# GpSimd joins the engines that keep the program's order in the attention loop of a transformer block

## The chip, the cores and the metric

The kernel runs on one core of one Trainium2 chip. The metric is the device time of one launch in microseconds (us); it is taken three times and the median counts. A core has five engines that run at the same time, each with an instruction queue of its own that it works through from front to back: TensorE (PE: matmuls and transposes, with PEld for its weight loads), VectorE (DVE), ScalarE (ACT), GpSimd (POOL) and SyncE (SP, which here only issues DMAs). Where one instruction needs another engine's result, it waits at the head of its queue for a semaphore, and all that stands behind it in that queue waits too.

## The reference

One transformer block on 1024 tokens of width 1024 in float32: a gated linear recurrence and a differential attention side by side, a projection of both, and an expert-choice mixture of experts. The part that this document is about is the attention and the projection behind it:

```python
def block(args):
    qi, start = args
    qpos = start + jnp.arange(Q_BLOCK, dtype=jnp.int32)
    bias = bias_table[t5_buckets(kpos[None, :] - qpos[:, None])].astype(jnp.float32)
    bias = bias.transpose(2, 0, 1)
    s = jnp.einsum('bqhjd,bkhjd->bhjqk', qi, k).astype(jnp.float32) + bias[None, :, None]
    p = jax.nn.softmax(s, axis=-1)
    w = (p[:, :, 0] - lam * p[:, :, 1]).astype(v.dtype)
    return jnp.einsum('bhqk,bkhd->bqhd', w, v)
...
o = rms_norm(o, g_o) * (1.0 - lam_init)
...
mix = jnp.dot(jnp.concatenate([y_lru, y_att], axis=-1), w_out[l])
x = x + gate1 * mix
```

There are 4 heads and 8 blocks of 128 queries for each, and two score matrices (j = 0, 1) for each block.

## The kernel before, in words

The program comes in stages: modulation and the first norm, input projections with the recurrence, the attention, the output projection with the second norm and the router's logits, the search for the experts' tokens, and the experts themselves. Float32 products are made of parts: an operand is split into a high part (ScalarE copies it) and a low part (the rest, by a subtraction), and TensorE multiplies the parts.

The attention loop (line 907 on) has NG + 2 = 34 iterations g. Its body is a software pipeline over 32 units (a unit is one head and one block of queries). In iteration g:

- TensorE transposes the weights of unit g-2 into two PSUM banks (`w_tr`, tile pw, line 814), multiplies the weights of unit g-3 with v (`pv_mm`, tile pv), and makes the scores of unit g+1 in two halves (`sc_mm`, tile sc), in the order pw, sc half 0, pv, sc half 1.
- VectorE adds the bias and finds the extremum of unit g's two halves (`sc_max`, line 768), and between them brings the two probability matrices of unit g-1 together (`comb0` line 798, `comb1` line 803, `comb2` line 807).
- ScalarE empties the two pw banks into tile wt (`w_evac`), and takes the two exponentials of unit g (`sc_exp`). `comb0` of a unit needs its second exponential, and the next transposes need the pw banks empty.

Every four units a tile of outputs is complete. `o_evac` (g = 6, 10, ...) has ScalarE copy it to tile o and GpSimd square it (osq, line 837). Two iterations later (g = 8, 12, ...) `o_rstd` has VectorE sum the squares (hov, line 845) and begin an inverse square root (hoy, lines 852 and 853), and GpSimd finish it with three Newton steps of four small instructions (hot and hoy, lines 855 to 858) and scale o with the result (line 861). At g = 10, 14, ... `o_out` transposes o on TensorE (tile po).

Into the same loop the preparation of the output projection is laid, one block k of 128 rows of w_out at g = 4, 8, 12, 16, 24, 26, 28 and 30 (`load_wo`): a DMA on SP's queue brings the block into a tile wo of a ring of five buffers, GpSimd multiplies it by the gate in four pieces (line 886), ScalarE copies the product to its high part (who, wx0o or wos, through `act`, line 90), and GpSimd subtracts that to get the low part (wlo, wx1o or wos, line 890). For the first tokens the projection starts in iteration 33, after the last scores.

What order an engine's instructions take is decided when the program is built. By default a scheduler goes by its own estimates of time and puts on each engine what it thinks is ready first. Within `tc.manual_schedule(engines=...)` the engines that are named take the order in which the Python code issues their instructions; here these are PE, DVE and ACT for the attention loop. GpSimd's and SP's instructions of the loop are placed by the scheduler.

Of the kernel before, what the change touches and what calls it, by code (L numbers as in the profile page):

```python
# [82 lines left out]
def tile_block(ctx: ExitStack, tc, x, cols, w_mod, b_mod, w_in, wa, wx, lam_qk, relT, w_out, g2, w_router,  # L83
# [639 lines left out]
    def prep_begin(h):  # L723
        sets = {}

        def load(tg, kind, parts):
            t_ = sets[tg] = qk_tile(f"{tg}{h}", F32R) if h else qk0[f"{tg}0"]
            for j in range(2):
                for a in range(2):
                    SY.dma_start(out=t_[j].bitcast(F32)[64 * a:64 * a + 64, :], in_=qkd[kind, h][parts[a], 64 * j:64 * j + 64, :])  # L730

        def bias():
            bt = sets["b"] = ap.tile([P, 1920], F32, name=f"bias{h}", tag="bias", bufs=1) if h % 2 else \
                qk_one("c", f"bias{h}", F32, [P, 1920]) if h else qk0["bias0"]
            src = bvd[h, 0:1920]
            SY.dma_start(out=bt, in_=bass.AP(tensor=src.tensor, offset=src.offset, ap=[[1, P], [1, 1920]]))

        qs, kh, kl = ("qs", 0, (0, 1)), ("kh", 1, (0, 0)), ("kl", 1, (1, 1))
        if h:
            for q in (qs, kh, kl):  # L740
                load(*q)
            bias()
        else:
            load(*kh)
            load(*kl)
            load(*qs)
            bias()
        prs[h] = (sets["b"], [sets[tg] for tg in ("qs", "kh", "kl")])
# [4 lines left out]
    def sc_mm(g, j):  # L753
        h, qt = divmod(g, NT)
        qs, kh, kl = (t_[j] for t_ in prs[h][1])
        sc_ = psa.tile([P, S], F32, tag="sc", bufs=2, name=f"sc{g}_{j}") if g > 1 else \
            psb.tile([P, S], F32, tag="pg", bufs=2, name=f"sc{g}_{j}")
        for i, kk in enumerate((kh, kl)):
            for n in range(2):
                mm(sc_[:, n * 512:(n + 1) * 512], qs[:, qt * P:(qt + 1) * P], kk[:, n * 512:(n + 1) * 512], i == 0, i == 1)  # L760
        scp[g, j] = sc_

    def sc_max(g, j):
        h, qt = divmod(g, NT)
        p_ = ap.tile([P, S], F32, tag="p", bufs=NPB, name=f"p{g}_{j}") if g > 1 else \
            raw_tile(f"p1_{j}", [P, S]) if g else p0[j]
        b0 = (NT - 1 - qt) * P
        V.tensor_tensor_reduce(out=p_, in0=scp[g, j], in1=prs[h][0][:, b0:b0 + S], op0=ALU.add, op1=ALU.min, scale=1.0,  # L768
                               scalar=3.0e38, accum_out=st_(g)[:, j:j + 1])
        pt_[g, j] = p_  # L770

    def sc_exp(g, j):
        h, qt = divmod(g, NT)
        act(pt_[g, j], pt_[g, j], AF.Exp, scale=-1.0, bias=st_(g)[:, j:j + 1], accum_out=s_sum[:, h, qt, j:j + 1])
# [21 lines left out]
    def comb0(g):  # L796
        h, qt = divmod(g, NT)
        V.reciprocal(out=st_(g)[:, 2:3], in_=s_sum[:, h, qt, 1:2])

    def comb1(g):  # L800
        h, qt = divmod(g, NT)
        r1 = st_(g)[:, 2:3]
        V.tensor_scalar(out=r1, in0=r1, scalar1=nlam, scalar2=s_sum[:, h, qt, 0:1], op0=ALU.mult, op1=ALU.mult)

    def comb2(g):
        r1 = st_(g)[:, 2:3]
        V.scalar_tensor_tensor(out=pt_[g, 0], in0=pt_[g, 1], scalar=r1, in1=pt_[g, 0], op0=ALU.mult, op1=ALU.add)

    def w_tr(g):
        for kq in range(2):  # L810
            pw = psa.tile([P, 512], F32, tag="pw", bufs=2, name=f"pw{g}_{kq}")
            for b in range(4):
                kt = kq * 4 + b
                T.transpose(pw[:, b * P:(b + 1) * P], pt_[g, 0][:, kt * P:(kt + 1) * P], ident)  # L814
            pvs[g, kq] = pw

    def w_evac(g):
        wts[g] = ap.tile([P, KT, P], F32, tag="wt", bufs=3, name=f"wt{g}")
        for kq in range(2):
            act(wts[g][:, kq * 4:kq * 4 + 4, :], pvs[g, kq].rearrange("p (b q) -> p b q", b=4))  # L820

    def pv_mm(g):
        n, i = divmod(g, 4)
        if i == 0:
            pvs["pv", n] = psa.tile([P, 4, P], F32, tag="pv", bufs=1, name=f"pv{n}")
        for kt in range(KT):
            mm(pvs["pv", n][:, i, :], wts[g][:, kt, :], vt[g // NT][:, kt, :], kt == 0, kt == KT - 1)
# [12 lines left out]
    def o_rstd(n):  # L840
        h, f = divmod(n, 2)
        o, sq = ots[n]
        v, t_, y = (xt_[f"ho{c}"] if n == 7 else ap.tile([P, 4], F32, tag=f"ho{c}", bufs=2, name=f"ho{c}{n}") for c in "vty")
        s0 = s_sum[:, h, f * 4:f * 4 + 4, 0]
        V.tensor_reduce(out=v, in_=sq, op=ALU.add, axis=AX.X)
        V.scalar_tensor_tensor(out=t_, in0=s0, scalar=EPS, in1=s0, op0=ALU.mult, op1=ALU.mult)
        V.scalar_tensor_tensor(out=v, in0=v, scalar=1.0 / P, in1=t_, op0=ALU.mult, op1=ALU.add)
        if h == NH - 1:
            act(y, v, AF.Sqrt)
            V.reciprocal(out=y, in_=y)  # L850
        else:
            V.tensor_scalar(out=y.bitcast(I32), in0=v.bitcast(I32), scalar1=1, scalar2=None, op0=ALU.logical_shift_right)
            V.tensor_scalar(out=y.bitcast(I32), in0=y.bitcast(I32), scalar1=-1, scalar2=0x5F3759DF, op0=ALU.mult, op1=ALU.add)
            for _ in range(3):
                G_.tensor_tensor(out=t_, in0=y, in1=y, op=ALU.mult)
                G_.tensor_tensor(out=t_, in0=t_, in1=v, op=ALU.mult)
                G_.tensor_scalar(out=t_, in0=t_, scalar1=-0.5, scalar2=1.5, op0=ALU.mult, op1=ALU.add)
                G_.tensor_tensor(out=y, in0=y, in1=t_, op=ALU.mult)
        for i in (slice(0, 4),) if h == NH - 1 else (slice(0, 2), slice(2, 4)):
            yb = y[:, i].unsqueeze(2).to_broadcast([P, i.stop - i.start, P])  # L860
            (V if h == NH - 1 else G_).tensor_tensor(out=o[:, i], in0=o[:, i], in1=yb, op=ALU.mult)
# [30 lines left out]
    def mix_mm(pm_, ns, k, yh, yl):  # L892
        mm(pm_, yh, woh[k][:, ns], k == 0, False)
        mm(pm_, yh, wol[k][:, ns], False, False)
        return mm(pm_, yl, woh[k][:, ns], False, k == KT - 1)
# [8 lines left out]
    gate1 = ap.tile([P, 1024], F32, name="gate1")  # L904
    src = modd[0][:, 0:1024]
    SY.dma_start(out=gate1, in_=bass.AP(tensor=src.tensor, offset=src.offset, ap=[[0, P], [1, 1024]]))
    with tc.manual_schedule(engines={mybir.EngineType.PE, mybir.EngineType.DVE, mybir.EngineType.Activation}):
        for g in range(NG + 2):
            hn, u = divmod(g, 8)
            if u == 0 and hn + 1 < NH:  # L910
                prep_begin(hn + 1)
            if g >= 2:
                w_tr(g - 2)
                w_evac(g - 2)
            if 1 < g < NG:
                sc_max(g, 0)
            if 1 <= g <= NG:
                comb0(g - 1)
            n, st = divmod(g - 8, 4)
            if st == 0 and 0 <= n < 6:  # L920
                o_rstd(n)
            if g < NG:
                if g > 1:
                    sc_exp(g, 0)
                if 0 < g < NG - 1:
                    sc_mm(g + 1, 0)
                if g > 1:
                    sc_max(g, 1)
            if 1 <= g <= NG:
                comb1(g - 1)  # L930
            if 1 < g < NG:
                sc_exp(g, 1)
            if 1 <= g <= NG:
                comb2(g - 1)
            if 3 <= g <= NG:
                pv_mm(g - 3)
            if g == NG:
                pv_mm(NG - 2)
            if 0 < g < NG - 1:
                sc_mm(g + 1, 1)  # L940
            if g in (4, 8, 12, 16, 24, 26, 28, 30):
                load_wo({4: 0, 8: 1, 12: 2, 16: 3, 24: 4, 26: 5, 28: 6, 30: 7}[g])
            n, st = divmod(g - 6, 4)
            if st == 0 and 0 <= n < 7:
                o_evac(n)
            n, st = divmod(g - 10, 4)
            if st == 0 and 0 <= n < 6:
                o_out(n)
            if g == NG + 1:
                o_rstd(6)  # L950
                mix0 = psa.tile([P, 1024], F32, tag="sc", bufs=2, name="mix0")
                for n in range(2):
                    ns = slice(n * 512, (n + 1) * 512)
                    for k in range(NCT):
                        mix_mm(mix0[:, ns], ns, k, y0[:, 0, k, :], y0[:, 1, k, :])
                o_out(6)
                pv_mm(NG - 1)
# [506 lines left out]
```

## Time and profile before

| | |
|---|---|
| median of 3 runs | 1181.63 us (1180.05 to 1181.79) |
| the profiled execution's own time | 1183.49 us |
| its span, first to last instruction | 1181.8 us |
| busy: PE, DVE, ACT, POOL | 1116.1, 955.8, 791.3, 481.7 us |
| attention loop in this span | about 315 to 475 us |
| experts in this span | from about 602 us on |

The span is what the profile shows; the time of the same execution is 1.7 us longer. A row of the timeline gives the start, the duration of a run of equal instructions, engine, line, operation, out<-in with the sizes, how many, and, in brackets, how long the engine had stood idle before and what ended that. Buffer numbers are left out of names there.

### The profile page before, as it was taken

The page shows a single profiled execution, that of the slowest core. Times are in us where ns is not written, and L with a number is a line of the kernel's source. Part 1 is how long each engine was busy: PE and PEld are TensorE (multiplying, and loading weights), DVE is VectorE, ACT ScalarE, POOL GpSimd, SP SyncE. Part 2 cuts the span into 40 slices and gives each one's busy share as a digit, 9 for nine tenths or more (in the row PEclk, how much of TensorE's full clock was granted, in tenths as well). Part 3 has the DMA queues.
Part 4 walks back from the last instruction along what each step waited for, and adds up shares of the span by engine and source line. Part 5 has one row for each costly group of instructions (what it writes and reads, how often), then busy time and mean ns, then how long its engine had stood idle before and what let it go on. Part 6 is the DMA issues. An engine that isn't in the chain of part 4 may idle for free.

```text
span 1181.8 us, 17872 instructions
## 1 busy us (share of the span) xinstructions
PE 1116.1 (94%) x6320; PEld 937.7 (79%) x6320; DVE 955.8 (81%) x1242; ACT 791.3 (67%) x1046; POOL 481.7 (41%) x540
## 2 busy tenths in 40 slices
PE   6999899999979999999569999999999999999996
PEld 4698898798869899777447888888888888888885
DVE  6897657875569896543679999999999999999995
ACT  7548282295467787543328887878888787888784
POOL 4693132133086646344534324444323444332400
PEclk9999999999999999999769999999999999999999
DMA  9765625704781505425799999999999999999911
GB/s 334 228 198 177 220 84 170 242 18 112 193 242 45 150 19 180 162 107 211 266 342 330 363 386 380 390 391 402 378 394 393 369 392 410 394 394 386 393 37 18
DMA packets 146994, 304.34 MB, mean 258 GB/s; under 512 B 16973, under 2 KB 43725, under 8 KB 146901
## 3 DMA queue, kind: packets, MB, share of 16 engines
q1 hardware_dynamic: 135008, 279.99, 65.7%
q0 software_dynamic: 5488, 19.45, 6.4%
q10 hardware_dynamic: 6408, 3.77, 1.1%
q8 instruction: 50, 0.82, 0.3%
q14 instruction: 40, 0.32, 0.1%
HBM read 277.95 MB, written 25.21 MB: 257 GB/s over the span
## 4 chain that ended last, share of the span: by engine, by line
PE 75%; DVE 7%; issue 5%; POOL 5%; DMA 5%; ACT 2%; SPq 1%; POOLq 0%; ACTq 0%; DVEq 0%
PE ab L93 28%; PE y L93 13%; PE mix L93 7%; PE pjz L93 4%; PE pjk L93 3%; PE sc L93 3%; PE pjv L93 3%; PE pv L93 3%; PE pw L814 2%; DMA wr<-in_w_mod_dram 2%; POOL wo L886 2%; PE pg L93 1%; DVE macc L623 1%; DMA wo<-in_w_out_dram 1%; PE pf L1348 1%
## 5 line engine op out<-in xcount | busy, mean ns | idle before, releaser
L1248 POOL TENSOR_SCALAR oh<-iot,slot 128x128 bf16<-128x128 bf16 x120 | 146.4, 1234 | 252.5 <-PE pf L1348 252.4
L93 PE MATMUL ab<-wh,xeh 128*128 128x512 f32 x512 | 202.2, 395 | 0.2 <-ACT xeh L90 0.2
L93 PE MATMUL ab<-wh,xel 128*128 128x512 f32 x512 | 199.7, 390 | 0.0
L93 PE MATMUL ab<-wl,xeh 128*128 128x512 f32 x512 | 157.7, 389 | 0.0
L93 PEld LDWEIGHTS ab<-wl,xeh 128*128 128x128 f32 x512 | 96.1, 188 | 20.4
L93 PEld LDWEIGHTS ab<-wh,xel 128*128 128x128 f32 x512 | 96.2, 188 | 19.5 <-DVE xel L1261 0.5
L93 PEld LDWEIGHTS ab<-wh,xeh 128*128 128x128 f32 x512 | 96.1, 188 | 19.5 <-ACT xeh L90 0.5
L141 DVE TENSOR_TENSOR wl<-w_0r,wh 128x1024 fp32r<-128x1024 f32 x79 | 96.8, 1226 | 10.2 <-ACT wh L90 0.4
L90 ACT ACTIVATE wh<-w_0r 128x1024 fp32r<-128x1024 f32 x81 | 86.1, 1062 | 24.8 <-PE ab L93 14.9
L141 DVE TENSOR_TENSOR wl<-w_3r,wh 128x1024 fp32r<-128x1024 f32 x79 | 96.7, 1225 | 6.2
L90 ACT ACTIVATE wh<-w_1r 128x1024 fp32r<-128x1024 f32 x79 | 83.5, 1058 | 23.7 <-PE ab L93 18.9
L90 ACT ACTIVATE wh<-w_3r 128x1024 fp32r<-128x1024 f32 x79 | 83.9, 1062 | 22.0 <-PE ab L93 17.4
L141 DVE TENSOR_TENSOR wl<-w_2r,wh 128x1024 fp32r<-128x1024 f32 x80 | 96.4, 1221 | 2.6 <-ACT wh L90 1.4
L90 ACT ACTIVATE wh<-w_2r 128x1024 fp32r<-128x1024 f32 x80 | 84.7, 1060 | 19.1 <-PE ab L93 18.7
L141 DVE TENSOR_TENSOR wl<-w_1r,wh 128x1024 fp32r<-128x1024 f32 x78 | 92.7, 1220 | 3.9 <-ACT wh L90 2.1
L768 DVE CUSTOM_DVE_ANT_0 p<-sc,bias 128x1024 f32<-128x1024 f32 x64 | 77.7, 1216 | 10.0 <-PE sc L93 9.9
L93 PE MATMUL y<-wh,htl 128*128 128x512 f32 x256 | 82.9, 395 | 0.0
L93 PE MATMUL y<-wh,hth 128*128 128x512 f32 x256 | 80.9, 396 | 0.0
L93 PE MATMUL y<-wl,hth 128*128 128x512 f32 x256 | 79.6, 391 | 0.0
L90 ACT ACTIVATE p<-p,stat 128x1024 f32<-128x1024 f32 x60 | 68.5, 1151 | 9.1 <-DVE stat L768 9.1
L93 PEld LDWEIGHTS pv<-v,wt 128*128 128x128 f32 x512 | 61.7, 192 | 2.5
L93 PE MATMUL pv<-v,wt 128*128 128x128 f32 x512 | 62.1, 275 | 0.0
(459 smaller groups left out, 2862.5 us busy)
## 6 DMA issues: line engine op xcount, KB each, us to landing
w_0r<-in_w_dram SPq DMA_DIRECT2D x81, 512.0 KB, 8.8
w_1r<-in_w_dram SPq DMA_DIRECT2D x79, 512.0 KB, 8.3
w_2r<-in_w_dram SPq DMA_DIRECT2D x78, 512.0 KB, 8.8
w_3r<-in_w_dram SPq DMA_DIRECT2D x77, 512.0 KB, 8.9
wr<-in_w_mod_dram SPq DMA_DIRECT2D x32, 512.0 KB, 4.9
wi<-in_w_in_dram SPq DMA_DIRECT2D x18, 512.0 KB, 4.4
w_5r<-in_w_dram SPq DMA_DIRECT2D x17, 512.0 KB, 8.0
wm<-in_w_mod_dram SPq DMA_DIRECT2D x32, 256.0 KB, 4.8
```

The lines of the kernel that those rows point to most:

```text
L90: return A.activation(out=out, in_=in_, func=func, **kw)
L93: return T.matmul(out, lhsT=lhsT, rhs=rhs, start=start, stop=stop)
L141: return (eng or V).tensor_tensor(out=lo, in0=src, in1=hi.bitcast(F32), op=ALU.subtract)
L623: V.scalar_tensor_tensor(out=macc[i], in0=w, scalar=sc[:, k:k + 1], in1=macc[i], op0=ALU.mult, op1=ALU.add)
L768: V.tensor_tensor_reduce(out=p_, in0=scp[g, j], in1=prs[h][0][:, b0:b0 + S], op0=ALU.add, op1=ALU.min, scale=1.0, scalar=3.0e38, accum_out ...
L814: T.transpose(pw[:, b * P:(b + 1) * P], pt_[g, 0][:, kt * P:(kt + 1) * P], ident)
L886: G_.tensor_tensor(out=r[:, qs], in0=r[:, qs], in1=gate1[:, qs], op=ALU.mult)
L1248: G_.tensor_scalar(out=oh[:, t, :], in0=iot, scalar1=slot[:, e, t:t + 1], scalar2=None, op0=ALU.is_equal)
L1348: T.transpose(pt[:, b * P:(b + 1) * P], sa[:, b * P:(b + 1) * P], ident)
```

## The change

GpSimd is added to the engines that keep the program's own order in the attention loop; nothing else is changed.

```diff
-    with tc.manual_schedule(engines={mybir.EngineType.PE, mybir.EngineType.DVE, mybir.EngineType.Activation}):
+    with tc.manual_schedule(engines={mybir.EngineType.PE, mybir.EngineType.DVE, mybir.EngineType.Activation, mybir.EngineType.Pool}):
         for g in range(NG + 2):
```

The orders of PE, DVE, ACT and SP are the same in both programs; GpSimd's differs in the attention loop alone. The first place is GpSimd's queue around its first work in the loop: the products with the gate (line 886) for blocks k = 0 to 5 (tiles wo0 to wo5), the low part of block 0 (wlo0), and the first squares (osq0); - is before, + is the change.

```order
 L886 TENSOR_TENSOR wo0_3164<-wo0_3164,gate1_3014 128x256 x4
-L886 TENSOR_TENSOR wo1_3385<-wo1_3385,gate1_3014 128x256 x2
 L890 TENSOR_TENSOR wlo0_3167<-wo0_3164,who0_3166 128x256 x4
-L886 TENSOR_TENSOR wo1_3385<-wo1_3385,gate1_3014 128x256 x2
-L886 TENSOR_TENSOR wo2_3593<-wo2_3593,gate1_3014 128x256 x4
-L886 TENSOR_TENSOR wo3_3820<-wo3_3820,gate1_3014 128x256 x4
-L886 TENSOR_TENSOR wo4_4222<-wo4_4222,gate1_3014 128x256 x4
-L886 TENSOR_TENSOR wo5_4315<-wo5_4315,gate1_3014 128x256 x4
 L837 TENSOR_TENSOR osq0_3258<-o0_3257 128x256 x2
 L855 TENSOR_TENSOR hot0_3340<-hoy0_3341 128x4
```

The products of blocks 1 to 5, twenty instructions, leave their place ahead of the first squares.

The second place is the same queue at g = 12, where the inverse square root of output tile 1 ends (line 858, then the scaling of o1) and block 2 is prepared.

```order
 L858 TENSOR_TENSOR hoy1_3549<-hoy1_3549,hot1_3548 128x4
 L861 TENSOR_TENSOR o1_3478<-o1_3478,hoy1_3549 128x256 x2
+L886 TENSOR_TENSOR wo2_3593<-wo2_3593,gate1_3014 128x256 x4
 L890 TENSOR_TENSOR wlo2_3596<-wo2_3593,who2_3595 128x256 x4
-L886 TENSOR_TENSOR wo7_4536<-wo7_4536,gate1_3014 128x256 x4
 L837 TENSOR_TENSOR osq2_3687<-o2_3686 128x256 x2
```

The product of block 2 now stands behind the Newton steps and the scaling of the same iteration, and that of block 7, which stood ahead of the squares of tile 2, is gone from here. At g = 8, 16, 24 and 28 it is alike with blocks 1, 3, 4 and 6; the products of 5 and 7 stand behind the low parts of 4 and 6.

The third place is ScalarE's queue at g = 12 and 13, the same in both programs: who2 reads the product of block 2.

```order
L90 ACTIVATE p12_0_3544,s_sum_2734<-p12_0_3544,stat_2998 128x1024
L90 ACTIVATE p12_1_3575,s_sum_2734<-p12_1_3575,stat_2998 128x1024
L90 ACTIVATE who2_3595<-wo2_3593 128x1024
L90 ACTIVATE wt11_3616<-pw11_0_3606 128x512
L90 ACTIVATE wt11_3616<-pw11_1_3611 128x512
L90 ACTIVATE p13_0_3619,s_sum_2734<-p13_0_3619,stat_2998 128x1024
L90 ACTIVATE p13_1_3628,s_sum_2734<-p13_1_3628,stat_2998 128x1024
```

Nothing moved here: behind who2 stand the emptying of the next pw banks and the exponentials of unit 13.

## Rows read from the trace of the kernel before

**Rows 1.** The page, part 4: the chain that ended last, shares by line.
```profile
PE ab L93 28%; PE y L93 13%; PE mix L93 7%; PE pjz L93 4%; PE pjk L93 3%; PE sc L93 3%; PE pjv L93 3%; PE pv L93 3%; PE pw L814 2%; DMA wr<-in_w_mod_dram 2%; POOL wo L886 2%; PE pg L93 1%; DVE macc L623 1%; DMA wo<-in_w_out_dram 1%; PE pf L1348 1%
```
**Rows 2.** Windows, undisturbed attention; stretch, its length, busy us by engine, clock, DMA.
```profile
400.00:420.00 20.00, 20.00 (x146) 18.38 (x145) 18.52 (x38) 15.97 (x30) 6.17 (x17) 1.00 0.09 28
```
**Rows 3.** Timeline, PE and ACT, g = 3 to 6: who0's wait.
```profile
329.84 1.06 ACT L90 ACTIVATE who<-wo 128x1024 fp32r<-128x1024 f32 x1 [1.80 <-POOL wo L886]
330.40 1.95 PE L93 MATMUL pv<-v,wt 128*128 128x128 f32 x16
...
334.16 0.16 DVE L798 RECIPROCAL stat<-s_sum 128x1 f32<-128x1 f32 x1 [1.43 <-ACT p L90]
...
334.92 1.95 PE L93 MATMUL pv<-v,wt 128*128 128x128 f32 x16
```
**Rows 4.** Timeline around g = 8: POOL, DVE, PE.
```profile
339.36 9.95 POOL L886 TENSOR_TENSOR wo<-wo,gate 128x256 f32<-128x256 f32 x13
...
344.17 1.95 PE L93 MATMUL pv<-v,wt 128*128 128x128 f32 x16
...
350.48 0.69 DVE L845 TENSOR_REDUCE hov<-osq 128x4 f32<-128x512 f32 x1 [7.40 <-POOL osq L837]
...
353.03 1.22 PE L93 MATMUL sc<-kh,qs 128*128 128x512 f32 x2 [6.91 <-DVE stat L768]
...
357.73 1.95 PE L93 MATMUL pv<-v,wt 128*128 128x128 f32 x16
```
**Rows 5.** Timeline around g = 16: DVE and PE.
```profile
389.65 0.69 DVE L845 TENSOR_REDUCE hov<-osq 128x4 f32<-128x512 f32 x1 [1.44 <-POOL osq L837]
...
390.19 1.95 PE L93 MATMUL pv<-v,wt 128*128 128x128 f32 x16
...
395.88 1.95 PE L93 MATMUL pv<-v,wt 128*128 128x128 f32 x16
```
**Rows 6.** Timeline, POOL, DVE and ACT in g = 11 to 13.
```profile
366.12 3.81 POOL L886 TENSOR_TENSOR wo<-wo,gate 128x256 f32<-128x256 f32 x4
...
370.78 0.17 DVE L853 TENSOR_SCALAR hoy<-hoy 128x4 int32<-128x4 int32 x1
...
373.77 1.05 ACT L90 ACTIVATE who<-wo 128x1024 fp32r<-128x1024 f32 x1
...
375.05 1.09 ACT L90 ACTIVATE wt<-pw 128x512 f32<-128x512 f32 x2 [0.23 <-PE pw L814]
...
375.40 1.19 POOL L861 TENSOR_TENSOR o<-o,hoy 128x256 f32<-128x256 f32 x2
```
**Rows 7.** Timeline, ACT, DVE and PE in g = 13 to 15.
```profile
377.15 1.14 ACT L90 ACTIVATE p<-p,stat 128x1024 f32<-128x1024 f32 x1
...
378.74 0.15 DVE L798 RECIPROCAL stat<-s_sum 128x1 f32<-128x1 f32 x1
378.93 1.04 PE L814 MATMUL pw<-ident,p 128*128 128x128 f32 x8
379.13 1.23 DVE L768 CUSTOM_DVE_ANT_0 p<-sc,bias 128x1024 f32<-128x1024 f32 x1 [0.25 <-PE sc L93]
...
380.28 0.27 DVE L803 TENSOR_SCALAR stat<-stat,misc,s_sum 128x1 f32<-128x1 f32 x1
...
380.59 1.29 DVE L807 SCALAR_TENSOR_TENSOR p<-p,stat,p 128x1024 f32<-128x1024 f32 x1
...
382.45 0.70 PE L93 MATMUL sc<-kh,qs 128*128 128x512 f32 x2
...
383.89 1.04 PE L814 MATMUL pw<-ident,p 128*128 128x128 f32 x8
```
**Rows 8.** Windows around gaps of PE; columns as in rows 2, PE busy third, clock after POOL.
```profile
36.40:39.20 2.80, 0.15 (x2) 0.08 (x1) 2.63 (x2) 0.38 (x1) 1.86 (x1) 1.00 1.15 343
39.60:42.90 3.30, 3.30 (x15) 2.07 (x15) 2.26 (x7) 2.48 (x2) 0.22 (x1) 0.50 1.00 324
...
350.20:357.00 6.80, 3.97 (x13) 3.38 (x14) 6.38 (x15) 2.94 (x5) 4.34 (x15) 0.50 0.62 184
...
390.00:394.00 4.00, 3.54 (x24) 2.81 (x23) 3.86 (x10) 3.00 (x6) 2.41 (x7) 1.00 1.04 245
```

## The prediction

> **What bounds the kernel now.** I read the page's chain first, then the attention by windows, then its timeline engine by engine. The chain is TensorE nearly all the way, but one entry of it is GpSimd's: the products with the gate, 2% of the span, with a load of w_out (1%) beside them [rows 1]. That is where the change acts. In an undisturbed part of the loop TensorE is busy for all 20.00 us of 20, VectorE for 18.52, ScalarE for 15.97 and GpSimd for 6.17 [rows 2]: TensorE is the bound, one unit takes 334.92 - 330.40 = 4.52 us from pv to pv [rows 3], and every gap that opens on TensorE here is lost for good, since the experts behind it are a chain of matmuls as well [rows 1].
>
> There are two such gaps now. At g = 8 GpSimd is in a run of gate products (13 of them from 339.36 on, 9.95 us), the first squares stand behind them, VectorE waits 7.40 us for these, and TensorE stands still for 6.91 us [rows 4]. From pv to pv that iteration takes 357.73 - 344.17 = 13.56 us. At g = 16 VectorE waits 1.44 us for squares behind the product of block 7, and the step is 395.88 - 390.19 = 5.69 us [rows 5].
>
> **What the change removes.** In the new order the first squares stand behind block 0 alone, and no squares of tiles 0 to 3 stand behind products of later blocks. Both waits go. Worth: 13.56 - 4.52 = 9.04 us and 5.69 - 4.52 = 1.17 us, together **10.2 us**. It is the same number of instructions on GpSimd; none is added, and no DMA moves, since SP's order is the same. The loads of blocks 6 and 7 wait on SP's queue for the low parts of blocks 1 and 2, which are a few us later relative to their units; behind them stand the keys of head 3, needed only at g = 23, and nothing else before the loop's end, so I cost that at nothing. If that cover were gone, a late key tile would stop the scores once, for a time like its own delay.
>
> **What it adds.** The scheduler had made the products long before ScalarE needs them. In the program's order the product of a block stands behind the Newton steps and the scaling of the same iteration, and these start only when VectorE has done its part (hoy). ScalarE's order is unchanged, so its copy who now reaches the head of its queue before the product exists, and behind it stand the emptying of the pw banks and both exponentials of the next unit. This is so at g = 8, 12, 16, 24 and 28, where a block and an inverse square root fall in one iteration: five times.
>
> One such wait, worked at g = 12 with the times that the rows have now. VectorE ends hoy at 370.95. GpSimd's Newton steps and scaling end at 375.40 + 1.19 = 376.59, and then come the four products, 3.81 us as in the group at 366.12: 380.40. ScalarE was ready for who2 at 373.77 [rows 6]. **It waits 6.6 us.** Then:
> - ScalarE: who2 to 381.45, then the two halves of wt, which began at 375.05: 6.4 us late [rows 6]. The second exponential of unit 13 started at 377.15 [rows 7], so now 383.55, and it ends at 384.7.
> - TensorE: its next transposes, at 378.93, need the first pw bank empty, now at 381.45 + 0.55 = 382.0 (half of 1.09): 3.1 us late [rows 6, 7].
> - VectorE: the reciprocal of unit 13, at 378.74, waits for that exponential: 384.75. Then the extremum, which at 379.13 had waited 0.25 us for TensorE, now runs to 386.1; line 803 (0.27) and line 807 (1.29) end at 387.7 [rows 7].
> - TensorE again: the scores at 382.45 need that extremum: 386.1, 3.7 us late; the transposes at 383.89 need line 807: 387.75, **3.9 us late** [rows 7]. The next scores wait another 0.3 us for VectorE, which has just 1.48 us in 20 to catch up with [rows 2]. So 4.2 us of TensorE are lost; 2.4 of the 6.6 are the lead that ScalarE and VectorE have over it.
>
> The one wait of this kind that the kernel has now fits: who0 waits 1.80 us for its product, VectorE loses 1.43 of that, and TensorE loses nothing (the step is those 4.52 us) [rows 3]. Five times 4.2 is **21.0 us**.
>
> *Both ends of that price.* If the four products run at the pace of the thirteen (9.95/13 x 4 = 3.06 us [rows 4]), a wait is 0.75 us shorter and costs 3.4; with half a us more lead, 3.0. Upward the clock comes in. TensorE's gap here is about 3.1 us in one piece. [...] I take 0.5 us for each wait, 2.5 in all, between 0 and 1.65 each.
>
> *The pairs at the end.* Blocks 5 and 7 come two iterations after 4 and 6, and their products stand behind the low parts of those. From hoy of g = 24: 9.45 to the product of block 4, 1.05 for its copy, 3.81 for its low part (as large as a product), 3.81 for the product of block 5: 18.1 us. ScalarE comes to that copy at 2.8 + 2 x 4.52 = 11.8, and 4.2 later for what was lost, 16.0. So it waits 2.1 us, with its lead already spent, and the emptying of the pv bank stands behind it. I take 1.5 us for each of the two, **3 us**, between 0 (as for who0) and 2.5.
>
> **The sum.** 21.0 + 2.5 + 3.0 - 10.2 = 16.3 us slower. The profiled execution took 1183.49 us, 1.86 more than the median of the runs; 16.3 on the median gives **1197.9 us**. Low end: 5 x 3.0 - 10.2 = 4.8, 1186.4 us. High end: 5 x (4.2 + 1.65) + 5 - 10.2 = 24.0, 1205.6 us.
>
> **The rivals.**
> - *The wait of ScalarE is absorbed.* Then only the gain is left: 1181.6 - 10.2 = 1171.4 us, faster. For it: who0's 1.80 us cost TensorE nothing [rows 3], and ScalarE has 4 us of 20 free [rows 2]. Against it: the lead is about 2.4 us, and a wait is 6.6. It decides at that lead: the Newton steps, scaling and product would have to take 5.2 us after hoy instead of 9.45, and the first 5.6 of these are in the trace [rows 6]. Chance 0.07.
> - *The clock falls after every one of the five waits and nothing hides it*: 5 x 1.65 instead of 2.5, and the pairs at 5 in all: 1205.6 us. For it: the gap of 2.65 us before 39.2 was enough [rows 8]. Against: TensorE waits for VectorE right behind the gap, slow or not. [...] Chance 0.13.
> - *The change cancels out*: each wait costs 2 us of TensorE, because VectorE and ScalarE have built up more lead after the first gap is gone than they have at g = 12. 5 x 2 - 10.2 = -0.2: 1181.4 us. For it: the loop's step at g = 8 has never been seen without its stall. Against: lead cannot grow past the two score buffers and two pw banks, and g = 12 has them full. Chance 0.05.
> That the change does nothing is no rival: GpSimd's order differs at the very places, as the order shows.
>
> **How the numbers follow.** Forecast 0.75, the clock 0.13, cancelling out 0.05, absorbed 0.07. A measurement of this kernel can tell about 0.2% from no change, 2.4 us. Faster by more than that: absorbed, 0.07. Within: most of the third rival, 0.03. Slower: 0.90. The range 1186.4 to 1206 takes in both ends of the unknown prices and the clock's rival; what is left out is the absorbed case, the cancelled one, and a little above.
>
> **What would show it.** In the profile after: no wait of VectorE for osq at g = 8 and 16, and step lengths there without the 13.56; ScalarE's who and wos waiting for line 886 five times for about 6 to 7 us, and two shorter ones; TensorE's transposes waiting for ScalarE, VectorE's reciprocal (line 798) for ScalarE about 6 us at a time; the loop longer by some 16 us, and all behind it shifted by as much. It is wrong if the waits for line 886 are there, but the steps of pv stay near 4.5 us (absorbed), or if they are not there, or if the experts take up the delay.

## The result, and the profile after

| | before | after |
|---|---|---|
| median of the runs | 1181.71 us (4 runs, 1180.05 to 1182.7) | 1195.76 us (4 runs, 1194.94 to 1196.83) |
| profiled execution, its span | 1183.49, 1181.8 us | 1195.35, 1193.6 us |

The change makes the kernel slower: after/before is 1.0121, with a 95% interval of 1.0103 to 1.0138, or 14.05 us on the medians. The forecast was 1197.9 us. One of the ten executions of experiment 3 took 3929.68 us, the others 1177.89 to 1181.44; it is left out of the ratio given there.

Where the time came from is read from pv to pv, the step of one unit. From the pv of unit 0 to that of unit 29 the loop took 141.65 us before (321.36 to 463.01) and takes 156.08 us now (318.85 to 474.93), **14.43 us more**. Behind that last pv the span has as much as before: 1181.8 - 463.01 = 718.8 us then, 1193.6 - 474.93 = 718.7 now. So the whole difference lies in the loop, where the prediction had put it.

The page's chain by lines, which answers to [rows 1]:

```profile
PE ab L93 28%; PE y L93 13%; PE mix L93 7%; PE pjz L93 4%; PE pjk L93 3%; PE pjv L93 3%; DMA wr<-in_w_mod_dram 2%; POOL wo L886 2%; DVE macc L623 2%; PE sc L93 2%; PE pv L93 1%; PE pjx L93 1%; ACT p L90 1%; PE pg L93 1%; PE pf L1348 1%
```

GpSimd's products stand there with the same 2% as before. The share doesn't tell the one case from the other: before it was one run of products at g = 8, now it is five pieces at five places. That is seen only in the waits and the timeline.

The waits of the loop in the kernel after (engine, tile and line that waits, what it waits for: us in total, times, longest):

```profile
ACT who L90 <- POOL wo L886: 15.0, 3, 6.7
...
ACT wos L90 <- POOL wo L886: 13.4, 2, 6.9
...
ACT wx0o L90 <- POOL wo L886: 6.5, 1, 6.5
...
DVE stat L798 <- ACT p L90: 32.9, 10, 5.9
...
DVE hov L845 <- POOL osq L837: 0.6, 1, 0.6
...
PE pw L814 <- ACT wt L90: 15.0, 5, 3.3
```

Six waits of ScalarE for line 886: who0 with about 1.8 us, as before [rows 3], and five of 6.5 to 6.9. Behind them VectorE waits for the exponential (up to 5.9 us at a time) and TensorE's transposes wait five times for the pw banks to be emptied, 15.0 us in all. The waits of VectorE for the squares, 7.40 and 1.44 us before [rows 4, 5], are gone; the one of 0.56 us that is left stands behind the low part of block 5 and was there before as well (0.56 us, at 445.52 of the trace before).

The stall of g = 8 first, in the timeline of after around it (columns as in the rows before: start, us, engine, line, operation; in brackets the idle time ahead and what ended it). The loop begins 2.5 us earlier in this execution than in that of [rows 4], so durations are to be compared, not times.

```profile
339.52 0.67 DVE L845 TENSOR_REDUCE hov<-osq 128x4 f32<-128x512 f32 x1
...
341.44 1.95 PE L93 MATMUL pv<-v,wt 128*128 128x128 f32 x16
...
345.96 1.95 PE L93 MATMUL pv<-v,wt 128*128 128x128 f32 x16
346.48 3.78 POOL L886 TENSOR_TENSOR wo<-wo,gate 128x256 f32<-128x256 f32 x4
350.29 1.06 ACT L90 ACTIVATE who<-wo 128x1024 fp32r<-128x1024 f32 x1 [6.67 <-POOL wo L886]
...
351.88 1.52 PE L814 MATMUL pw<-ident,p 128*128 128x128 f32 x8 [3.04 <-ACT wt L90]
...
354.91 2.43 PE L93 MATMUL pv<-v,wt 128*128 128x128 f32 x16
```

VectorE sums the squares at 339.52 with no wait, and the step is 345.96 - 341.44 = 4.52 us, where it was 13.56 [rows 4]. One step later the new stall comes: the product ends at 350.26, who1 had stood before it for 6.67 us, and from pv to pv it is 354.91 - 345.96 = 8.95 us.

The same at g = 12, the place that the prediction worked out from [rows 6, 7], in the timeline of after:

```profile
363.95 0.17 DVE L853 TENSOR_SCALAR hoy<-hoy 128x4 int32<-128x4 int32 x1
...
368.58 1.19 POOL L861 TENSOR_TENSOR o<-o,hoy 128x256 f32<-128x256 f32 x2
...
369.37 1.95 PE L93 MATMUL pv<-v,wt 128*128 128x128 f32 x16
369.73 3.78 POOL L886 TENSOR_TENSOR wo<-wo,gate 128x256 f32<-128x256 f32 x4
...
373.54 1.06 ACT L90 ACTIVATE who<-wo 128x1024 fp32r<-128x1024 f32 x1 [6.50 <-POOL wo L886]
...
375.13 1.15 PE L814 MATMUL pw<-ident,p 128*128 128x128 f32 x8 [2.90 <-ACT wt L90]
...
377.57 3.02 PE L93 MATMUL pv<-v,wt 128*128 128x128 f32 x16
...
377.85 0.16 DVE L798 RECIPROCAL stat<-s_sum 128x1 f32<-128x1 f32 x1 [5.86 <-ACT p L90]
...
383.59 1.95 PE L93 MATMUL pv<-v,wt 128*128 128x128 f32 x16
```

Read it as a chain: hoy ends at 364.12, Newton steps and scaling at 369.77, the four products at 373.51. That is 9.39 us after hoy (forecast 9.45). ScalarE's copy has waited 6.50 us (6.6), the transposes 2.90 (3.1), VectorE's reciprocal 5.86 (about 6). The two steps behind it are 8.20 and 6.02 us. Without a stall they would be 4.52 and 4.95 (the second carries the transposes of line 869), 9.47 in all, so this place loses 4.75 us.

All five places, by the same sum (at g = 28 the two steps without a stall are 4.51 + 4.02 = 8.53 us):

| g | ScalarE waits | TensorE's gap | two steps | lost | clock behind the gap |
|---|---|---|---|---|---|
| 8 | 6.67 | 3.04 | 8.95 + 5.44 | 4.92 | fell |
| 12 | 6.50 | 2.90 | 8.20 + 6.02 | 4.75 | fell |
| 16 | 6.52 | 2.93 | 7.72 + 5.88 | 4.13 | stayed |
| 24 | 6.50 | 2.91 | 7.68 + 6.50 | 4.71 | stayed |
| 28 | 6.94 | 3.26 | 8.46 + 5.21 | 5.14 | fell |

Together 23.65 us lost. Won are 13.56 - 4.52 = 9.04 at g = 8, 5.69 - 4.50 = 1.19 at g = 16 and 0.20 at g = 6, 10.4 in all. 23.65 - 10.4 leaves 13.2 of the 14.43; the other 1.2 us are at the end of the loop, a step of 5.25 us for 4.95 (g = 28) and one of 3.65 for 2.73 (the last).

The clock behind the five gaps, by windows of after (stretch, its length, busy us of PE, PEld, DVE, ACT and POOL with the instructions, then the granted clock; [rows 8] before):

```profile
352.60:355.90 3.30, 3.30 (x13) 2.91 (x12) 1.30 (x4) 3.30 (x7) 1.62 (x3) 0.50 0.17 50
376.40:379.80 3.40, 3.40 (x15) 3.12 (x14) 1.91 (x5) 3.40 (x8) 1.07 (x2) 0.50 0.24 80
396.00:402.00 6.00, 3.62 (x28) 3.36 (x28) 0.89 (x2) 5.21 (x10) 3.56 (x6) 1.00 0.24 75
436.60:442.00 5.40, 2.55 (x18) 2.31 (x19) 0.00 (x0) 4.14 (x7) 4.23 (x7) 1.00 0.02 5
465.20:468.50 3.30, 3.30 (x15) 3.09 (x14) 2.00 (x5) 3.30 (x9) 3.30 (x6) 0.50 0.35 87
```

It was 0.50 of full speed behind three of the five gaps and 1.00 behind the other two. Where it is low, sixteen pv matmuls take 3.02 us for 1.95, as at 377.57 above.

### The profile page after: what moved, and what is told of

The parts are those of the page before. It is cut to its first block, busy times and chain, and to the rows that moved or that the text cites. A ratio compares the mean times of both kernels' runs of the same rounds, so it can differ in the third digit from the quotient of the medians.

```text
span 1193.6 us, 17866 instructions
## 1 busy us (share of the span) xinstructions
PE 1118.3 (94%) x6320; PEld 938.6 (79%) x6320; DVE 954.6 (80%) x1242; ACT 790.4 (66%) x1046; POOL 476.8 (40%) x540
## 3 DMA queue, kind: packets, MB, share of 16 engines
q10 hardware_dynamic: 6408, 3.77, 1.1%
## 4 chain that ended last, share of the span: by engine, by line
PE 71%; DVE 8%; POOL 6%; issue 5%; DMA 5%; ACT 4%; SPq 0%; POOLq 0%; ACTq 0%; DVEq 0%
PE ab L93 28%; PE y L93 13%; PE mix L93 7%; PE pjz L93 4%; PE pjk L93 3%; PE pjv L93 3%; DMA wr<-in_w_mod_dram 2%; POOL wo L886 2%; DVE macc L623 2%; PE sc L93 2%; PE pv L93 1%; PE pjx L93 1%; ACT p L90 1%; PE pg L93 1%; PE pf L1348 1%
## 5 line engine op out<-in xcount | busy, mean ns | idle before, releaser
L141 DVE TENSOR_TENSOR wl<-w_0r,wh 128x1024 fp32r<-128x1024 f32 x79 | 96.8, 1226 | 10.2 <-ACT wh L90 0.4
L93 PEld LDWEIGHTS pv<-v,wt 128*128 128x128 f32 x512 | 64.9, 200 | 2.8
L93 PE MATMUL pv<-v,wt 128*128 128x128 f32 x512 | 64.9, 282 | 0.0
```

Source lines behind the costliest of these rows:

```text
L93: return T.matmul(out, lhsT=lhsT, rhs=rhs, start=start, stop=stop)
L141: return (eng or V).tensor_tensor(out=lo, in0=src, in1=hi.bitcast(F32), op=ALU.subtract)
```

## The experiments

The theory: ScalarE's copy waits for a product that stands behind the Newton steps and the scaling in GpSimd's queue; what that wait has over a lead of some 2.4 us TensorE loses, five times. The rivals: the copy's place or GpSimd's total work is to blame, not the product's place; or the five waits are a symptom and the loss lies elsewhere.

**1. All products ahead of the Newton steps.** load_wo is cut in two: the load and the product go ahead of o_rstd in the same iteration, the copy and the low part stay where they were.

```diff
+            if k is not None:
+                load_wo(k)
             n, st = divmod(g - 8, 4)
             if st == 0 and 0 <= n < 6:
                 o_rstd(n)
...
-            if g in (4, 8, 12, 16, 24, 26, 28, 30):
-                load_wo({4: 0, 8: 1, 12: 2, 16: 3, 24: 4, 26: 5, 28: 6, 30: 7}[g])
+            if k is not None:
+                split_wo(k)
```

> GpSimd stays in the program's order, but the gate products of a block are issued ahead of the inverse square root of the same iteration, where before they stood behind it. ScalarE's queue stays as it is. Theory (ScalarE's copy waits at its queue's head for a product that stands behind the Newton steps): the five waits for line 886 at g = 8, 12, 16, 24 and 28 are gone, and with them the 23.6 us that these steps lost in the changed kernel; the squares stay early, so the waits that the kernel before had do not come back. 1195.8 - 23.6 = 1172 us, between 1169 and 1175. Rival (the loss comes from GpSimd's work being spread over the loop, through its ports or the clock, wherever it stands): it stays above 1188 us.

Measured: 1175.73 us (1172.96 to 1177.7), 0.9953 [0.9939, 0.9968] of before's 1181.07, and 20.0 us under the changed kernel. All five waits are gone, and with them the gaps of 2.9 us: the loop takes 135.75 us for 156.08. The same instructions run on GpSimd, and only the place of the products among them was changed (their loads are issued earlier too; in the changed kernel GpSimd waits for one load of w_out alone, that of block 0, 12.6 us), so the first rival (the copy's place, or the amount of work) falls. It is 3.7 us over the forecast, and the steps say where: at g = 28 one takes 7.68 us, for 4.95 in the kernel before, and two steps later comes one of 5.40 for 4.02. The timeline of both places, VectorE, GpSimd, ScalarE and TensorE of this kernel (GpSimd's product is line 888 here):

```profile
434.21 2.77 POOL L888 TENSOR_TENSOR wo<-wo,gate 128x256 f32<-128x256 f32 x4
434.27 0.69 DVE L845 TENSOR_REDUCE hov<-osq 128x4 f32<-128x512 f32 x1 [0.54 <-POOL osq L837]
434.88 0.76 DVE L846 SCALAR_TENSOR_TENSOR hot<-s_sum 128x4 f32<-128x4 f32 x1
435.67 0.65 DVE L847 SCALAR_TENSOR_TENSOR hov<-hov,hot 128x4 f32<-128x4 f32 x1
436.35 0.65 DVE L852 TENSOR_SCALAR hoy<-hov 128x4 int32<-128x4 int32 x1
...
438.40 0.74 PE L93 MATMUL sc<-kh,qs 128*128 128x512 f32 x2 [2.05 <-DVE stat L768]
...
450.41 1.06 ACT L90 ACTIVATE wos<-wo 128x1024 fp32r<-128x1024 f32 x1 [1.62 <-POOL wo L888]
...
452.00 2.05 PE L93 MATMUL pv<-v,wt 128*128 128x128 f32 x16 [1.21 <-ACT o L90]
```

VectorE is late already (the squares end late behind the low part of block 5, and the exponential 2.0 us late), and its three small instructions of four elements take 2.06 us beside GpSimd's product. TensorE waits 2.05 us for the extremum behind them. The second place is a wait that the changed kernel does not have: ScalarE's copy of block 7 waits 1.62 us for the product, which stands behind the low part of block 6, the emptying of the pv bank stands behind that copy, and TensorE waits 1.21 us for the bank. (The copy of block 5 waits 1.25 us.)

**2. Only the product of block 1 moved** (the same edit, with the condition k == 1 for the early place, so that the other products stay with their copies).

> As the run with all products first, but for block 1 (g = 8) alone. Theory: one of five stalls is gone, 4.9 us by the steps of pv at g = 8 in the changed kernel: 1190.9 us, and the four others keep their length. Rival (the loop has slack elsewhere, so that what is saved at one place is waited out at the next): 1195 us as the changed kernel.

Measured: 1191.55 us (1190.12 to 1192.04), 1.0085 [1.0072, 1.0098], 4.2 us under the changed kernel; its loop takes 151.17 us for 156.08, which is 4.91 less. The steps at g = 8 are 4.50 and 4.96, the wait of who1 is gone, and the four others stay with 6.5, 6.8, 6.5 and 6.5 us. A wait that is taken away gives back its own price (4.92 at g = 8 in the table) and no more.

This run is also the one that prices the clock, since its falls lie elsewhere. Windows behind its gaps at g = 12, 16, 24 and 28:

```profile
371.00:374.50 3.50, 3.23 (x23) 2.65 (x22) 3.10 (x6) 3.50 (x9) 0.00 (x0) 1.00 0.70 226
391.10:394.60 3.50, 3.05 (x12) 2.78 (x13) 0.33 (x2) 3.50 (x7) 2.78 (x4) 0.51 0.00 0
432.20:438.80 6.60, 5.75 (x23) 5.36 (x24) 2.99 (x5) 6.60 (x13) 5.54 (x8) 0.50 0.24 84
462.00:466.00 4.00, 3.43 (x27) 2.80 (x25) 4.00 (x7) 4.00 (x9) 2.16 (x4) 1.00 0.97 336
```

At g = 12 both kernels wait 6.5 us and have a gap of 2.9; here the clock stays and 7.68 + 5.89 - 9.47 = 4.10 us are lost, there it fell and 4.75 were: 0.65 for the fall. At g = 24 it is the other way round: a gap of 2.91 us in both, 9.25 + 6.10 - 9.47 = 5.88 here with the fall (0.50 in all of the 6.6 us of the window), 4.71 there without: 1.17. At g = 16 and 28 the two kernels differ in the wait as well. At g = 16 it is 9.32 + 4.95 - 9.47 = 4.80 here with the fall and 4.13 there without, and the wait is 0.30 us longer here; at g = 28 it is 5.14 there with the fall and 7.62 + 5.49 - 8.53 = 4.58 here without, and the wait is 0.47 us longer there. Less the wait that leaves about 0.4 and 0.1. So a fall cost between 0.1 and 1.2 us.

**3 and 7. A shorter and a longer wait.** The loop over Newton steps makes one or five in place of three for heads 0 to 2; nothing moves.

```diff
-            for _ in range(3):
+            for _ in range(1):
```

> The changed kernel with one Newton step where there were three; two of the three steps of the inverse square root of heads 0 to 2 are left out. Eight small instructions of 0.28 us, with or without one long one of 1.2 us, come out of the stretch between hoy and the product, so a wait of 6.5 us becomes 3.3 to 4.3 us. Theory (ScalarE and VectorE have a lead of about 2.2 us, and what is over it is lost): each stall costs 1.1 to 2.1 us where it cost 4.7; five of them save 13 to 18 us: 1178 to 1183 us. Rival (a fixed share of every wait is lost, 4.7 of 6.5): each costs 2.4 to 3.1 us, 1184 to 1188 us.

> The changed kernel with five Newton steps where there were three. Eight small instructions of 0.28 us, with or without one long one of 1.2 us, are added ahead of the product: a wait of 6.5 us becomes 8.8 to 9.8 us. Theory (all that is over the lead of 2.4 us is lost): a stall costs 6.4 to 7.4 us and some more where the clock falls, against 4.7: 8.5 to 16 us over the changed kernel, 1204 to 1212 us. Rival (a longer wait is taken in elsewhere): under 1202 us.

Measured: one step 1179.62 us, 0.9985 [0.9975, 0.9995]; five steps 1209.93 us (1208.59 to 1210.32), 1.0237 [1.0221, 1.0253] of before's 1181.79. One row of ScalarE's waits of each (g = 16), first with one step, then with five:

```profile
ACT wx0o L90 <- POOL wo L886: 3.6, 1, 3.6
```

```profile
ACT wx0o L90 <- POOL wo L886: 8.8, 1, 8.8
```

| Newton steps | each wait | lost at each place | clock |
|---|---|---|---|
| 1 | 3.3 to 3.7 | 0.95 to 1.51, mean 1.2 | stayed at g = 8, 12 and 16 (transposes behind the wait 1.06 to 1.07 us) |
| 3 (the changed kernel, g = 16) | 6.5 | 4.1 | stayed there |
| 5 | 8.8 to 9.2 | 6.91 to 8.25, mean 7.6 | fell at g = 8, 12 and 16 (transposes 1.97 us for 1.03) |

At g = 12 and 16 one step leaves 3.57 - 0.99 and 3.59 - 0.96, about 2.6 us, and three steps leave 6.49 - 4.10 (experiment 2) and 6.52 - 4.13, 2.4 us: the lead that was worked out from [rows 6, 7]. (With one step, steps of 4.68 to 4.74 us for 4.51 follow at g = 12, 16 and 20; they are not counted in.) At g = 24 the lead is smaller, 3.27 - 1.51 and 6.50 - 4.71, 1.8 us with either length. So where the clock stayed, the price follows the length of the wait, about one for one above the lead, and the rivals fall that a fixed share of the wait is lost or that the loss lies elsewhere. With five steps a lead of 2.4 would leave 6.5 of 8.9 us; the other 1.1 would fit the falls of the clock, but at g = 8, 12 and 16 this run has no wait without a fall that would show it.

**4. The copy two iterations later.** Products as in the changed kernel; copy and low part of each block two iterations behind them.

```diff
+            k = {4: 0, 8: 1, 12: 2, 16: 3, 24: 4, 26: 5, 28: 6, 30: 7}.get(g - 2)
+            if k is not None:
+                split_wo(k)
```

> GpSimd's products stay where the changed kernel has them, behind the Newton steps; ScalarE's copy of a block and GpSimd's low part move two iterations later, so ScalarE no longer reaches the copy before the product is there. Theory (what costs is that the copy blocks the head of ScalarE's queue, not that the product is late): all five stalls go, 1172 us, between 1169 and 1176. Rival (the product's lateness itself or GpSimd's contention is what costs): no more than a few us better than 1195.8.

Measured: 1177.2 us (1175.0 to 1179.25), 0.9969 [0.9957, 0.9982]; 5 us over the forecast. The five waits go here too, from the other end; two short ones, 0.81 and 2.37 us, are left at the loop's end and behind it. But a low part now stands ahead of the squares in GpSimd's queue, and ahead of the squares that are summed at g = 28 the product of block 5 as well, and VectorE waits for squares six times, most of all at g = 28 (a step of 8.60 us). Timeline of this kernel, GpSimd and VectorE there:

```profile
429.44 3.81 POOL L895 TENSOR_TENSOR wos<-wo,wos 128x256 fp32r<-128x256 f32 x4 [3.52 <-ACT wos L90]
433.21 2.82 POOL L888 TENSOR_TENSOR wo<-wo,gate 128x256 f32<-128x256 f32 x4
435.98 1.19 POOL L837 TENSOR_TENSOR osq<-o 128x256 f32<-128x256 f32 x2
...
437.21 0.69 DVE L845 TENSOR_REDUCE hov<-osq 128x4 f32<-128x512 f32 x1 [3.36 <-POOL osq L837]
```

It is the kind of wait that the kernel before had at g = 8, made by other work.

**5. Products in GpSimd's idle iterations.** As in 1, but each product is issued where GpSimd has nothing due, and at g = 26 and 30 the output tile's copy and squares go ahead of the block's copy and low part.

```diff
+            for k in {4: (0,), 7: (1,), 11: (2,), 15: (3,), 18: (4,), 19: (5,), 21: (6,), 22: (7,)}.get(g, ()):
+                load_wo(k)
...
             if st == 0 and 0 <= n < 7:
                 o_evac(n)
+            if k is not None:
+                split_wo(k)
```

> GpSimd in the program's order, with each product issued in an iteration in which GpSimd stands idle (g = 7, 11, 15, 18, 19, 21, 22 for blocks 1 to 7), so that none stands beside the inverse square root; at g = 26 and 30 the output tile's copy and squares are issued ahead of the block's copy and low part. Theory: no wait of VectorE for squares and no wait of ScalarE for line 886 but who0's; both gains (9.0 and 1.2 us, and 0.5 at g = 28) stay and no loss is added: 1181.1 - 10.7 = 1170.4 us, between 1168 and 1173, and the steps of pv are 4.5 or, with the transposes of o, 4.95 all along. Rival (something else than the place of the products still binds at the end of the loop): 1173 to 1176 us as the run with the products first.

Measured: 1171.92 us (median of 5; 1170.83 to 1176.7), 0.9917 [0.9904, 0.9931]. It **beats both kernels**, by 9.9 and 23.8 us, with all four engines still in the program's order; the loop takes 130.65 us, for 141.65 before and 156.08 in the changed kernel. One row is left of ScalarE's waits for a product, that of who0:

```profile
ACT who L90 <- POOL wo L888: 1.7, 1, 1.7
```

The steps are 4.50 to 4.52 us and, with line 869, 4.95; no gap of TensorE in the loop is over 0.9 us. It is the time that the prediction's rival "absorbed" gave (1171.4 us), reached by taking the waits away and not by hiding them. What its two edits give apart, the earlier products and the squares ahead of the low part, was not tried.

**6. The old stall brought back.** As 5, but the products of blocks 1 to 5 all at g = 5, ahead of the first squares, as the scheduler had them.

```diff
+            for k in {4: (0,), 5: (1, 2, 3, 4, 5), 21: (6,), 22: (7,)}.get(g, ()):
+                load_wo(k)
```

> As the run with products in GpSimd's gaps, but the products of blocks 1 to 5 are all issued at g = 5, ahead of the first squares, as the scheduler had them. Theory (the first term of the prediction): the stall at g = 8 comes back alone, 9.0 us in the step of pv from g = 8 to 9: 9 us over the run with products in gaps, 1179 to 1180 us. Rival (VectorE's wait at g = 8 has another cause than these products, such as the loads of the keys that run at the same time): no stall at g = 8, the same time as the run with products in gaps.

Measured: 1181.55 us (1179.25 to 1185.3), 0.9993 [0.9978, 1.0008], 9.6 us over experiment 5. Timeline of this kernel, GpSimd, VectorE and TensorE:

```profile
337.42 10.65 POOL L888 TENSOR_TENSOR wo<-wo,gate 128x256 f32<-128x256 f32 x14
...
342.23 1.95 PE L93 MATMUL pv<-v,wt 128*128 128x128 f32 x16
...
349.24 0.69 DVE L845 TENSOR_REDUCE hov<-osq 128x4 f32<-128x512 f32 x1 [8.10 <-POOL osq L837]
...
356.83 1.95 PE L93 MATMUL pv<-v,wt 128*128 128x128 f32 x16
```

The step of g = 8 is 14.60 us, with 8.10 us of VectorE's wait, and the kernel is back at the time of before. So the products ahead of the squares are enough to make the stall of [rows 4]; the loads move along with them in this edit, but fourteen of the products take 10.65 us, 0.76 each, in one run without a wait. It is worth 9.6 us on the medians and 14.60 - 4.52 = 10.1 in the step, where the prediction had 9.0 and this run's forecast 1179 to 1180 us.

## Why the prediction was right, point by point

- *What is removed, 10.2 us*: right. The steps at g = 8 and 16 are without their stalls, 9.04 + 1.19, and experiment 6 gets the first back (10.1 us) by putting the products ahead of the squares again.
- *The loads, costed at nothing*: right. In the loop of after GpSimd waits for a load of w_out once, for block 0 (12.6 us, as before), and TensorE for no tile of keys.
- *Five waits of 6.6 us*: right, 6.50 to 6.94. The chain behind hoy took 9.39 us for 9.45, and who waits for whom is as it was worked out, row for row.
- *4.2 us of TensorE for each, 2.4 absorbed*: right. Where the clock stayed it was 4.10 (g = 12, experiment 2), 4.13 (g = 16), 4.71 (g = 24) and 7.62 + 5.49 - 8.53 = 4.58 (g = 28, experiment 2); waits of 3.6 and 6.5 us at g = 12 and 16 give 2.4 to 2.6 us of lead. The places late in the loop lose half a us more with either length of wait (1.8 us of lead at g = 24); why was not tried.
- *The clock, 0.5 for each, 2.5 in all*: right in sum, wrong in kind, and the sum came out in part by luck. It is not half a us at each wait: no run shows a price of 0.5 for every wait, nor one of 1.65 (half of a stretch of 3.3 us) for a fall. The clock stayed at two of the five, and a fall cost between 0.1 and 1.2 us. Five times 4.2 + 0.5 is 23.5; measured 23.65. But of the 2.65 us above 21.0, 0.51 lie at g = 24, where the clock stayed, and 0.38 at g = 28 would be there without a fall too (4.58 in experiment 2). The rival that it falls at all five and costs 1.65 each was wrong in both parts. What the prediction said against it, that TensorE waits for VectorE behind the gap "slow or not", holds at full clock alone: there it waits 0.26 us (g = 16) and 0.27 and 0.57 (g = 24), while in the slow stretches of after it was busy throughout (3.30 of 3.30 us, 3.40 of 3.40, 3.30 of 3.30). So half the clock takes the place of a wait that would have come, which hides part of its price; how the rest of it adds up was not worked out.
- *The pairs at the end, 3.0 us*: **this term was mis-sized**, and it makes most of the 2.1 us between 1197.9 and 1195.76. Measured are 1.2 us at the end of the loop, and none of them comes from a wait of blocks 5 or 7, so the waits that the term priced cost nothing. GpSimd and ScalarE around block 5, and TensorE at the last step, timeline of after:

```profile
438.99 2.80 POOL L890 TENSOR_TENSOR wos<-wo,wos 128x256 fp32r<-128x256 f32 x4 [1.17 <-ACT wos L90]
441.75 2.81 POOL L886 TENSOR_TENSOR wo<-wo,gate 128x256 f32<-128x256 f32 x4
...
445.26 1.06 ACT L90 ACTIVATE wos<-wo 128x1024 fp32r<-128x1024 f32 x1
...
474.03 1.06 PE L814 MATMUL pw<-ident,p 128*128 128x128 f32 x8 [0.80 <-DVE p L807]
```

  The prediction had low part and product at 3.81 us each and so 18.1 us from hoy to the end of the product. They took 2.80 and 2.81, and the product ended 444.56 - 428.43 = 16.1 us behind hoy (which ends at 428.43). ScalarE came 16.8 us behind hoy (forecast 16.0): two steps with 4.2 us lost would be 13.24 us, and they took 7.68 + 6.50 = 14.18. It waits for nothing. The wait itself is no invention: in experiment 1, where ScalarE is not held up, it is there with 1.25 and 1.62 us, and the second costs TensorE 1.21. The term rested on one duration of a group of four where the rows showed two paces, 3.81 and 3.06, and took the long one at every step. Of the 1.2 us, 0.92 are in the last step, where TensorE's last transposes wait 0.80 us for VectorE. That step takes 3.21 to 3.77 us in the four kernels with the stall at g = 28 (after and experiments 2, 3 and 7) and 2.71 to 2.77 in the other five, so it goes with that stall, which is the last and costs this on top of its two steps. Where the other 0.30 come from (the step of 5.25 us at g = 28, with a wait of 0.29 us for line 807) is open; VectorE's wait of 0.56 us for squares there is the same as before.
- *The rivals.* Absorbed: no, for the reason given, a lead of 2.4 us against a wait of 6.5. Cancelling out: no, the lead did not grow when the first stall was gone; g = 8 loses as much as g = 12.
- *All behind the loop shifted by as much*: right; the experts took up none of it.

## What to carry to other kernels

When an engine is put into the program's order, list for each consumer at the head of another in-order queue what now stands between it and its producer, and price the wait as (its length minus the lead of the engines between); here 6.5 - 2.4, five times over, and half a us more late in the loop, where the lead is smaller. The program's order is not at fault, only the line on which a producer is issued: work with no deadline of its own (the products) goes into iterations in which its engine has nothing due, behind what is due soon and well ahead of its reader, and the same manual order then goes from 1195.8 to 1171.9 us. A share of the chain that stays the same (2% for line 886 here) can hide that a wait has moved and multiplied.

## What the runs showed of the hardware

- *Small VectorE instructions beside GpSimd.* In experiment 1 three VectorE instructions on 128x4 elements (lines 846, 847 and 852) took 0.76, 0.65 and 0.65 us while GpSimd ran four float32 products; the same three take 0.15, 0.16 and 0.17 in after, where GpSimd stands still at that moment:

```profile
340.11 0.15 DVE L846 SCALAR_TENSOR_TENSOR hot<-s_sum 128x4 f32<-128x4 f32 x1
340.29 0.16 DVE L847 SCALAR_TENSOR_TENSOR hov<-hov,hot 128x4 f32<-128x4 f32 x1
340.49 0.17 DVE L852 TENSOR_SCALAR hoy<-hov 128x4 int32<-128x4 int32 x1
```

  In experiment 1 they end at 435.64, 436.32 and 437.00; at the mean pace of the group, 2.77/4 = 0.69 us, the second, third and fourth product would end at about 435.6, 436.3 and 437.0. That is an estimate from the group's duration. What makes the three long no run here shows.
- *Long GpSimd instructions.* Among equal ones some take 1.0 us more. In the Newton steps of g = 24 one of twelve took 1.22 us, the others 0.19 or 0.20; a group of four products takes 2.8 or 3.8 us:

```profile
429.92 1.22 POOL L856 TENSOR_TENSOR hot<-hot,hov 128x4 f32<-128x4 f32 x1
```

  Two of them lie in the chain of 9.39 us at g = 12. What makes them is open; they decided whether block 5 would wait: its product ended 16.1 us behind hoy with neither of them in the low part and the product, with both it would have been 18.1, behind ScalarE's 16.8.
- *The clock after equal gaps.* Behind gaps of 2.83 to 3.26 us it fell five times and stayed four times, in after and experiment 2 together; the three over 3.0 us all brought a fall, of the six from 2.83 to 2.93 us two did. Behind the gaps of 5.45, 5.14 and 5.19 us of experiment 7 (g = 8, 12 and 16) the transposes took 1.97 us for 1.03, as they did in experiment 2 at g = 16, where the clock was 0.51. At g = 12 after's fell and experiment 2's did not, with 2.90 and 2.89 us of gap, and in after it was still 1.00 from 375.2 to 376.4, with TensorE at work again since 375.13, and 0.50 only from there to 379.8. What decides between them no run here shows.
- *Left open too*: that the profiled loop of after began 2.5 us earlier than that of before, with the same order ahead of it, was not followed up. In the nine profiled executions of all kernels the loop's first pv lies between 317.4 and 324.2 us. The time behind the loop was the same, and the medians differ by 14.05 us, close to the 14.43 of the loop.
